# Batch norm in inference form: load and store phases of three tiles in place of two

## The chip, the cores and the metric

The kernel runs on one core of a Trainium2 chip. The metric is the device time of one execution in microseconds (us). The profile's span is about 2 us shorter than the device time of the same execution. The differences that matter are a few tenths of a per cent, so every kernel was run five times or more, beside runs of the kernel before on the same chip. The batches ran on different chips, so kernels of different batches are compared by their ratios to before, or by their traces, and not by their medians.

## The reference

```python
# x: (32, 256, 128, 128) float32; the rest: 256 float32 each
out = gamma * (x - running_mean) / np.sqrt(running_var + 1e-5) + beta
```

The input and the output are 537 MB each. There is one multiply and one add per element, with one scale and one shift per channel.

## The kernel before

The data is cut into 64 tiles of 128 partitions by 16,384 float32 (8.39 MB, 64 KiB in each partition). There are three such buffers. VectorE works on a tile in place.

```python
NBUF = 3
...
    data = ctx.enter_context(tc.tile_pool(name="data", bufs=NBUF))
...
    for i in range(NBUF):
        issue_load(i)                 # nc.sync.dma_start(out=t, in_=xr[i])
    ...                               # scale and shift from the four small inputs
    def compute(i):
        nc.vector.tensor_scalar(out=t[:], in0=t[:], scalar1=scale_t[:, cb:cb+1],
            scalar2=shift_t[:, cb:cb+1], op0=mult, op1=add)      # cut
    def store(i):
        (nc.sync if SINGLE_QUEUE else nc.scalar).dma_start(out=outr[i], in_=t[:])

    K = NBUF - 1
    for b in range((NT + K - 1) // K):
        idxs = [i for i in range(K * b, K * b + K) if i < NT]
        for i in idxs:
            compute(i)
        for i in idxs:
            store(i)
        for i in idxs:
            issue_load(i + NBUF)
```

Loads and stores share one queue, issued by SyncE (`SINGLE_QUEUE` is true). So the DMA engines see three loads, then two stores, two loads, two stores and so on. Each place where a store follows a load in the queue is called a load-to-store switch here; the kernel before has 32.

## Time and profile before

| | before |
|---|---|
| device time, median of the first 3 runs (5 in the end) | 2487.14 us (2487.04) |
| range of the 5 runs | 2486.45 to 2490.18 us |
| the run that was profiled | 2490.18 us, the slowest of them |
| HBM traffic, mean rate | 1073.8 MB, 432 GB/s |

From the page of the profile (kernel before): busy time of the compute engines, then the span in 40 slices with the busy share in tenths and the rate, then the DMA queue.

```profile
DVE 564.7 (23%) x69; ACT 1.6 (0%) x2; POOL 3.2 (0%) x8
...
DMA  9999999999999999999999999999999999999998
GB/s 414 429 438 433 433 429 437 436 430 431 435 436 433 428 437 436 434 428 436 433 437 428 435 435 435 426 437 436 435 427 435 436 438 426 434 437 436 432 431 378
...
q1 hardware_dynamic: 18432, 1073.75, 99.8%
```

VectorE is busy 23% of the time. The DMA engines are busy all the time, but for a little in the last slice. This is a copy with a little arithmetic in its shadow, and its time is that of its 128 tile transfers.

From the timeline of the kernel before (SyncE's queue; start, length, line, what was issued; a load is issued when the store of that buffer has landed):

```profile
82.93 19.66 SPq L48 DMA_DIRECT2D t<-in_x_dram  x2
102.63 28.19 SPq L97 DMA_DIRECT2D out_dram<-t  x2
160.34 19.61 SPq L48 DMA_DIRECT2D t<-in_x_dram  x2
180.00 28.16 SPq L97 DMA_DIRECT2D out_dram<-t  x2
238.40 19.62 SPq L48 DMA_DIRECT2D t<-in_x_dram  x2
...
2409.84 0.34 SPq L48 DMA_DIRECT2D t<-in_x_dram  x1
```

Between 82.93 and 2409.84 lie 30 rounds of two stores and two loads: 77.56 us each.

From its waits (waiter, released by: us in total, times, longest):

```profile
DVE t L86 <- DMA t<-in_x_dram: 1867.9, 63, 49.6
...
SPq L48 <- DMA out_dram<-t: 1484.0, 61, 30.2
SPq L97 <- DVE t L86: 919.2, 33, 46.4
```

VectorE waits three quarters of the time and SyncE nearly all of it. That costs nothing as long as another transfer is queued behind the one that is running.

The trace also records every DMA packet (start and length). Each tile transfer is 8 packets of 64 KiB on each of the 16 DMA engines, and one 4-byte semaphore packet per engine at its end. The records do not name the engine, but on an engine the next packet starts when the last ends, so they can be chained into 16 series (some of the 18,432 links are ambiguous). An undisturbed packet takes 2.418 us for loads and stores alike, and an undisturbed transfer starts 19.319 us after the one before it. That is 8.389 MB / 19.319 us = 434.2 GB/s, next to the 435.2 GB/s that the Trainium skill gives as the ceiling of the SBUF ports, by which these engines reach the on-chip memory ("DMA: Bandwidth & Descriptors", section "Where 436 GB/s comes from").

### The profile page before, as it was taken

Reading aid. Unit: us, or ns where it says so; the run is one execution under the profiler, and the core shown is the slowest. Engines: PE = TensorE matmul, PEld = TensorE weight load, DVE = VectorE, ACT = ScalarE, POOL = GpSimd, SP = SyncE. Lnnn points to the kernel's source line nnn. Section 1 sums busy time; section 2 is a strip of 40 time slices with the busy share of each in tenths; the row PEclk is TensorE's granted clock in tenths of the full one; section 3 lists DMA queues with packets and bytes.
Section 4 is the critical chain, followed back from the end, with each engine's and each line's share of the span. In section 5 each row is a group of like instructions: output and inputs, shape, how many; then the busy total and the mean of one; then the engine's idle time right before and its main releaser. Section 6 shows DMA issues by size and latency. Waiting matters only on the chain.

```text
span 2488.1 us, 378 instructions
## 1 busy us (share of the span) xinstructions
DVE 564.7 (23%) x69; ACT 1.6 (0%) x2; POOL 3.2 (0%) x8
## 2 busy tenths in 40 slices
DVE  2122211222112221122212222121221212212121
ACT  0000000000000000000000000000000000000000
POOL 0000000000000000000000000000000000000000
DMA  9999999999999999999999999999999999999998
GB/s 414 429 438 433 433 429 437 436 430 431 435 436 433 428 437 436 434 428 436 433 437 428 435 435 435 426 437 436 435 427 435 436 438 426 434 437 436 432 431 378
DMA packets 18562, 1073.77 MB, mean 432 GB/s; under 512 B 2176, under 2 KB 2176, under 8 KB 2176
## 3 DMA queue, kind: packets, MB, share of 16 engines
q1 hardware_dynamic: 18432, 1073.75, 99.8%
q0 software_dynamic: 128, 0.00, 0.0%
q14 instruction: 2, 0.02, 0.0%
HBM read 536.88 MB, written 536.87 MB: 432 GB/s over the span
## 4 chain that ended last, share of the span: by engine, by line
DMA 51%; another core or an unknown queue 36%; DVE 11%; SPq 0%; issue 0%; POOL 0%; DVEq 0%; POOLq 0%; PEldq 0%
DMA t<-in_x_dram 48%; DVE t L86 11%; DMA out_dram<-t 2%; DMA t<-in_running_mean_dram 1%; SPq L97 0%; POOL t L56 0%; DVEq L86 0%; POOLq L133 0%; SPq L48 0%; DVE shift_t L81 0%; DVE tmp_t L80 0%; DVEq L80 0%; PEldq L133 0%
## 5 line engine op out<-in xcount | busy, mean ns | idle before, releaser
L86 DVE TENSOR_SCALAR t<-t,scale_t,shift_t 128x16384 f32<-128x16384 f32 x64 | 564.0, 8812 | 1868.0 <-DMA t<-in_x_dram 1867.9
L78 DVE RECIPROCAL tmp_t<-tmp_t 128x2 f32<-128x2 f32 x1 | 0.2, 166 | 13.2 <-ACT tmp_t L71 13.2
L80 DVE TENSOR_TENSOR tmp_t<-t,scale_t 128x2 f32<-128x2 f32 x1 | 0.2, 160 | 7.6 <-DMA t<-in_running_mean_dram 7.6
L71 ACT ACT_TABLE_LOAD x1 | 1.3, 1283 | 12.4 <-DMA t<-in_running_var_dram 12.4
L79 DVE TENSOR_TENSOR scale_t<-t,tmp_t 128x2 f32<-128x2 f32 x1 | 0.2, 160 | 3.2 <-DMA t<-in_gamma_dram 3.2
L56 POOL DMA_DIRECT2D t<-in_running_var_dram x1 | 0.8, 839 | 0.8 <-PEq L133 0.8
L56 POOL DMA_DIRECT2D t<-in_gamma_dram x1 | 0.7, 722 | 0.0
L56 POOL DMA_DIRECT2D t<-in_beta_dram x1 | 0.7, 722 | 0.0
L56 POOL DMA_DIRECT2D t<-in_running_mean_dram x1 | 0.7, 722 | 0.0
L71 ACT ACTIVATE tmp_t<-t,eps_t 128x2 f32<-128x2 f32 x1 | 0.3, 295 | 0.0
L65 DVE MEMSET eps_t<- 128x1 f32 x1 | 0.1, 59 | 0.8 <-PEq L122 0.8
L81 DVE TENSOR_TENSOR shift_t<-t,tmp_t 128x2 f32<-128x2 f32 x1 | 0.2, 160 | 0.0
L122 POOL MEMSET const-bfloat16-1.0<- 128x1 bf16 x1 | 0.1, 96 | 0.0
L122 POOL MEMSET const-uint8-127<- 128x1 uint8 x1 | 0.1, 94 | 0.0
L122 POOL MEMSET const-float32-0.0<- 128x1 f32 x1 | 0.1, 93 | 0.2 <-issue 0.2
L122 POOL MEMSET const-float32-1.0<- 128x1 f32 x1 | 0.1, 93 | 0.0
## 6 DMA issues: line engine op xcount, KB each, us to landing
t<-in_x_dram SPq DMA_DIRECT2D x64, 38.6
out_dram<-t SPq DMA_DIRECT2D x64, 49.9
t<-in_running_var_dram POOLq DMA_DIRECT2D x1, 1.0 KB, 11.1
t<-in_gamma_dram POOLq DMA_DIRECT2D x1, 1.0 KB, 15.2
t<-in_beta_dram POOLq DMA_DIRECT2D x1, 1.0 KB, 19.5
t<-in_running_mean_dram POOLq DMA_DIRECT2D x1, 1.0 KB, 21.6
```

Source lines behind the costliest of these rows:

```text
L56: nc.gpsimd.dma_start(out=t, in_=ap_1d.rearrange("(j p) -> p j", p=P))
L65: nc.vector.memset(eps_t, eps)
L71: nc.scalar.activation(out=tmp_t[:], in_=var_t[:], func=mybir.ActivationFunctionType.Sqrt, bias=eps_t[:], scale=1.0,)
L78: nc.vector.reciprocal(out=tmp_t[:], in_=tmp_t[:])
L79: nc.vector.tensor_mul(out=scale_t[:], in0=gamma_t[:], in1=tmp_t[:])
L80: nc.vector.tensor_mul(out=tmp_t[:], in0=mean_t[:], in1=scale_t[:])
L81: nc.vector.tensor_sub(out=shift_t[:], in0=beta_t[:], in1=tmp_t[:])
L86: nc.vector.tensor_scalar(out=t[:], in0=t[:], scalar1=scale_t[:, cb : cb + 1], scalar2=shift_t[:, cb : cb + 1], op0=mybir.AluOpType.mult, ...
L122: nc = _bacc.Bacc("TRN2", target_bir_lowering=False, num_devices=1)
```

## The change

The intent: fewer changes of direction. All three buffers are loaded, then all three are stored; 22 load-to-store switches in place of 32. Loads, computes, stores, buffers and the queue stay, and `manual_schedule` keeps the instructions in the order written.

```diff
-SINGLE_QUEUE = True
 NBUF = 3
+GROUPS = [3] * 20 + [2, 2]
...
+    ctx.enter_context(tc.manual_schedule())
...
-    K = NBUF - 1
-    for b in range((NT + K - 1) // K):
-        idxs = [i for i in range(K * b, K * b + K) if i < NT]
+    first = 0
+    for g, size in enumerate(GROUPS):
+        idxs = range(first, first + size)
         for i in idxs:
             compute(i)
         for i in idxs:
             store(i)
-        for i in idxs:
-            issue_load(i + NBUF)
+        first += size
+        if g + 1 < len(GROUPS):
+            for i in range(first, first + GROUPS[g + 1]):
+                load(i)
```

More of the change, by code (lines that the diff above doesn't have):

```diff
@@ L33 @@
     NT = N * NCB
+    assert sum(GROUPS) == NT and max(GROUPS) <= NBUF
     params = ctx.enter_context(tc.tile_pool(name="params", bufs=1))
@@ L39, with load @@
     outr = out.rearrange("n (cb p) h w -> (n cb) p (h w)", p=P)
+    ctx.enter_context(tc.manual_schedule())
     tiles = {}
-    loads = {}
-    def issue_load(i):
-        if i >= NT:
-            return
+    def load(i):
         t = data.tile([P, HW], mybir.dt.float32, tag="t")
-        loads[i] = nc.sync.dma_start(out=t[:], in_=xr[i])
+        nc.sync.dma_start(out=t[:], in_=xr[i])
         tiles[i] = t
-    for i in range(NBUF):
-        issue_load(i)
+    for i in range(GROUPS[0]):
+        load(i)
     def load_param(ap_1d):
@@ L96, in store @@
         t = tiles.pop(i)
-        (nc.sync if SINGLE_QUEUE else nc.scalar).dma_start(out=outr[i], in_=t[:])
-    K = NBUF - 1
-    for b in range((NT + K - 1) // K):
-        idxs = [i for i in range(K * b, K * b + K) if i < NT]
+        nc.sync.dma_start(out=outr[i], in_=t[:])
+    first = 0
+    for g, size in enumerate(GROUPS):
+        idxs = range(first, first + size)
         for i in idxs:
@@ L105 @@
             store(i)
-        for i in idxs:
-            issue_load(i + NBUF)
+        first += size
+        if g + 1 < len(GROUPS):
+            for i in range(first, first + GROUPS[g + 1]):
+                load(i)
 _INS = ['x', 'gamma', 'beta', 'running_mean', 'running_var']
```

## The prediction

> **What bounds the kernel now.** The DMA engines. The page gives DMA 9 tenths in 39 of 40 slices, queue q1 99.8% of the 16 engines' span, 432 GB/s mean; VectorE is 23% busy. The Trainium skill, "DMA: Bandwidth & Descriptors", section "Where 436 GB/s comes from", puts the ceiling at 435.2 GB/s; the trace agrees to 1% (inner slices of 426 to 438).
>
> From the trace's DMA packet records: 16,384 packets of 64 KiB, median 2.418 us each, the same for loads and stores; one 8.39 MB tile takes 19.32 us from start to start. 128 transfers x 19.32 = 2473 us. The span is 2488.1, so only about 15 us (0.6%) is anything else: about 2 us before the first packet, about 1 us of slow first packets, small delays, the last completion.
>
> **The avoidable part.** Times over 2.418 us sit almost all at one place: the end of the last load of a phase and the start of the store behind it (summed per engine, 1.6 us over 31 last loads, 2.3 us over 32 first stores). Store-to-load switches show 0.1 us. In wall time (timeline): the first load of a phase is issued at 82.93 and, 30 rounds of two stores and two loads later, at 2409.84: 77.56 us a round, against 4 x 19.32 = 77.28. So about 0.29 us is lost per load-to-store switch.
>
> **What the change does.** The work stays: 64 loads, 64 computes (8.81 us each), 64 stores, same buffers, same queue. By the instruction order, load-to-store switches fall from 32 to 22. Ten x 0.29 = about 2.9 us (estimate), all on the critical path since the DMA engines are.
>
> The fear is a drain, because all three buffers are now loaded before any is stored. I expect none. When the third load lands, two stores are already queued behind it: their computes ended while loads of 19.3 us still ran. The third compute (8.81 us) hides under those stores (38.6 us). When the first store lands, two more are queued while its load is issued; before, one was. The skill, same page, section "Queues, rings and completion order", says each engine consumes descriptors in ring order; the trace agrees (landings 19.3 us apart). The deeper queue also tolerates drift between engines (their last packets end about 9 us apart), worth a microsecond or two at most. VectorE's longest waits grow from 49 to about 68 us and cost nothing. Start and tail stay.
>
> **Prediction.** 2487.1 - 2.9 = 2484.2 us; 8 in 10 between 2481.0 and 2487.2. Faster by over 2%: 0.005 (the floor of 2473 us is only 0.6% away); same: 0.985; slower by over 2%: 0.01.
>
> **What would show it.** Right: DMA still 9 in every slice but the last, mean GB/s up by 0 to 1; VectorE still 564 us; a period of 6 transfers of 115.9 plus about 0.3 us between the first loads of phases; packet excess still only at load-to-store switches, a third fewer. Wrong: a period of 116.5 us or more says the cost goes with the length of a phase, not the number of switches; a slice with DMA well under 9 would be a bubble.
>
> **What would make it wrong.** A cost per switch that grows with the phase's length; the fixed program order adding a wait on SyncE; long phases letting the engines drift further apart, so that the slowest engine's tail eats the gain; run-to-run spread (2486.6 to 2490.2 before) as large as the effect.

## The result, and the profile after

| | before | after |
|---|---|---|
| median of 5 runs | 2487.04 us | 2488.37 us |
| range | 2486.45 to 2490.18 | 2486.35 to 2490.49 |
| the run that was profiled | 2490.18 (span 2488.1) | 2487.72 (span 2485.7) |

The ratio is 1.0003, with a 95% interval of 0.9991 to 1.0016. A ratio is the mean time of one kernel's runs over that of the other's of the same rounds, so it is not quite the ratio of the medians. The gain of 0.12% that was predicted is not there, and the median lies 1.2 us above the predicted range.

From the page of the kernel after:

```profile
DVE 564.7 (23%) x69; ACT 1.6 (0%) x2; POOL 3.2 (0%) x8
...
DMA  9999999999999999999999999999999999999999
GB/s 408 436 439 429 431 438 430 435 435 432 429 438 436 432 431 436 436 427 436 436 432 432 436 437 428 433 438 431 430 439 436 427 437 438 430 431 438 436 432 390
...
q1 hardware_dynamic: 18432, 1073.75, 99.8%
```

No slice ran dry: the feared drain is not there. VectorE's work is the same.

From the timeline of the kernel after (SyncE's queue):

```profile
82.67 39.17 SPq L46 DMA_DIRECT2D t<-in_x_dram  x3
149.65 38.99 SPq L95 DMA_DIRECT2D out_dram<-t  x3
198.75 39.07 SPq L46 DMA_DIRECT2D t<-in_x_dram  x3
...
2291.51 19.66 SPq L46 DMA_DIRECT2D t<-in_x_dram  x2
```

From 82.67 to 2291.51 there are 19 rounds of three stores and three loads, 116.25 us each.

From its waits:

```profile
DVE t L84 <- DMA t<-in_x_dram: 1865.8, 63, 69.0
...
SPq L95 <- DVE t L84: 1455.0, 64, 47.2
SPq L46 <- DMA out_dram<-t: 949.7, 60, 19.1
```

VectorE's longest wait grew from 49.6 to 69.0 us, as foreseen, at no cost.

Now a trap. Taken alone, the two profiles seem to confirm the prediction: 2488.1 us fell to 2485.7, which is 2.4 of the 2.9 us. But the profile of before is that of its slowest run, and that of after is of one of its faster ones. The other runs show no gain.

### The profile page after: what moved, and what is told of

It reads as the page before. It is cut to its first block, busy times and chain, and to the rows that moved or that the text cites. A ratio compares the mean times of both kernels' runs of the same rounds, so it can differ in the third digit from the quotient of the medians.

```text
span 2485.7 us, 377 instructions
## 1 busy us (share of the span) xinstructions
DVE 564.7 (23%) x69; ACT 1.6 (0%) x2; POOL 3.2 (0%) x8
## 4 chain that ended last, share of the span: by engine, by line
another core or an unknown queue 72%; DVE 22%; DMA 4%; issue 0%; DVEq 0%; SPq 0%
DVE t L84 22%; DMA t<-in_x_dram 4%; DVEq L84 0%; SPq L46 0%; SPq L95 0%
```

## The experiments

Fifteen runs of five or six executions each were made, two of them repeats. The theories:

- **A**: every load-to-store switch costs a fixed 0.2 to 0.3 us (the prediction's view), and the first runs were unlucky.
- **B**: the loss goes with bytes or time, not with switches.
- **C**: the fixed program order costs what the switches gain.
- **D**: a switch costs more after a longer phase.
- **E** (formed after the first four runs): the 16 engines start in step; at switches some of them fall behind; once they have drifted apart, further switches cost little. The time is that of the engine furthest behind.
- **F**: the delays fade with time or addresses, not with drift.

### How many switches: 1, 8, 32 and 62

Run `alternate`: one load, one store, in turn.

```diff
-    first = 0
-    for g, size in enumerate(GROUPS): ...
+    compute(0); compute(1); store(0); store(1)
+    for i in range(2, NT):
+        if i + 1 < NT:
+            load(i + 1)
+        compute(i)
+        store(i)
```

> One load, one store, in turn after the first three loads: 62 load-to-store switches in place of 32, same work. Theory A (each switch costs a fixed 0.2 to 0.3 us): +6 to +9 us over before. Theory B (the loss is there per byte or per microsecond of the run, whatever the number of switches): within 1.5 us of before. Theory C (the fixed program order costs the 3 us that the change failed to gain): this kernel has it too, so +3 to +4 us, plus A or B.

Measured: median 2486.71 us (2485.27 to 2488.95), ratio to before 0.9999 (0.9986 to 1.0013). The interval allows at most 3.2 us for thirty more switches, where A asked for 6 to 9: A is wrong as it stands, and the +3 us of C is not seen.

Runs `phase8` and `phase64`: within a phase each buffer is loaded and computed several times, and only its last contents are stored, into every output. Their outputs are wrong, which doesn't matter for the times. The transfers and the VectorE work are the same in number and size.

```diff
-    first = 0 ...
+    first = 0
+    for size in GROUPS:                  # [8] * 8, or [64]
+        idxs = range(first, first + size)
+        for k, i in enumerate(idxs):
+            load(i)                      # into bufs[i % NBUF]
+            if k >= NBUF - 1:
+                compute(i - NBUF + 1)
+        for i in list(idxs)[-(NBUF - 1):]:
+            compute(i)
+        for i in idxs:
+            store(i)                     # from bufs[i % NBUF], in phase64 (i + 1) % NBUF
+        first += size
```

> Phases of eight loads and eight stores through the three buffers (wrong result on purpose), 8 load-to-store switches in place of 32. Theory A: 24 fewer switches, -5 to -7 us against before. Theory B: within 1.5 us of before. A third theory, D (a switch costs more the longer the phase before it): also about 0, and the excess over the bare 2.418 us packet time per switch is several times that of before.

> All 64 loads (each computed), then 64 stores: one load-to-store switch (wrong result on purpose). Theories A and D: -6 to -9 us, near 2479 to 2481 us, and the run-to-run spread shrinks from 4 us to about 1. Theory B: within 1.5 us of before with the same spread, and slow packets everywhere in the trace.

Measured: `phase8` 2484.26 us (2483.90 to 2485.42), ratio 0.9989 (0.9976 to 1.0001); `phase64` 2484.44 us (2484.14 to 2484.64), ratio 0.9988 (0.9976 to 1.0001). The intervals just reach 1, but all ten runs lie below the fastest of the nine runs of before beside them (2486.46). Even with one switch only about 3 us go (0.12% of 2487), and 6 us at most, not the 6 to 9 of A; B, which expected a change of at most 1.5 us, misses too. D expected no gain from `phase8`, and its delay at the last loads was 0.07 us per switch, less than in the kernel before: D falls. The spread of `phase64` shrank to 0.5 us, so with one switch the scatter is nearly gone.

Run `two_fixed`: the kernel before with `manual_schedule` added, nothing else.

```diff
+    ctx.enter_context(tc.manual_schedule())
     tiles = {}
```

> The kernel before with the fixed program order alone, phases of two as they were. Theories A, B and D: the same as before within 1.5 us. Theory C: +3 us or more.

Measured: 2487.21 us (2485.58 to 2488.74), ratio 1.0000 (0.9987 to 1.0012). The +3 us or more of C is not there (the interval ends at +3.0 us).

### Repeats of both kernels

> The changed kernel once more, for its spread and a second trace. Theory A (a fixed 0.2 to 0.3 us per load-to-store switch, first five runs unlucky): median near 2484.5. Theory E (the loss comes while the 16 engines drift apart from their common start, mostly in the first ten or so switches, and is not per switch): 2486 to 2489, as before; in the trace the last load packet before a store is late by about 0.15 to 0.2 us per engine in each of the first ten switches and less than that in the last ten.

Measured: 2487.91 us (2487.12 to 2488.54), ratio to before 0.9992 (0.9978 to 1.0005). Over both batches the changed kernel's ten runs have a mean of 2488.25 us. But the chip of this batch was slower (before had a median of 2488.92 us there), and the interval holds the predicted 0.9988: this batch alone does not separate A from E. Against before on the same chip the means of the changed kernel differ by +1.2 us in the first batch and by -1.8 us here. So a gain of about a microsecond is not excluded. The part of the expectation on fading fails within this kernel: the delays of the last loads sum to 1.43 us per engine over the first ten switches and to 1.40 over the last ten.

Run `three_sched` is the changed kernel with the `manual_schedule` line taken out.

```diff
-    ctx.enter_context(tc.manual_schedule())
     tiles = {}
```

> The changed kernel without the fixed program order. All theories that leave the order aside (A, E): the same as the changed kernel within 1.5 us. Theory C (the fixed order costs): 3 us less.

Measured: 2488.04 us (2486.51 to 2490.61), ratio to before 0.9995 (0.9982 to 1.0007), as with it (its mean is 1.1 us under that of before on this chip). No effect of the order shows.

> The kernel before once more, for a second trace. If the 0.29 us per round of the first profile is typical: (period of two stores and two loads) again 77.55 to 77.60 us. If it was the mark of a slow run: 77.40 to 77.50 us, that is 0.1 to 0.2 us per switch, and lag of the slowest engine at the end 4 to 7 us in place of 9.2. In both cases the delays of the first ten switches are larger than those of the last ten.

Measured: 2487.12 us (2486.58 to 2491.17), ratio 1.0001 (0.9989 to 1.0013). This time the profiled run was a short one, 2486.58 us. From its timeline (SyncE's queue):

```profile
82.71 19.75 SPq L48 DMA_DIRECT2D t<-in_x_dram  x2
...
2406.74 0.34 SPq L48 DMA_DIRECT2D t<-in_x_dram  x1
```

Thirty rounds in 2324.03 us are 77.47 us each, against 77.56 in the first profile. So a switch cost 0.19 us here, not 0.29. The timeline gives for all six profiles of the two orders (loss is the period less 4 or 6 times 19.319 us):

| run | period, us | lost per switch | times its switches |
|---|---|---|---|
| before (profiled run 2490.18) | 77.564 | 0.29 | 32: 9.2 |
| before_again (2486.58) | 77.468 | 0.19 | 32: 6.1 |
| two_fixed (2487.21) | 77.486 | 0.21 | 32: 6.7 |
| after (2487.72) | 116.255 | 0.34 | 22: 7.5 |
| after_again (2487.91) | 116.257 | 0.34 | 22: 7.5 |
| three_sched (2487.99) | 116.278 | 0.36 | 22: 8.0 |

This is the answer to the main question. Fewer switches cost more each, and the product stays at 6 to 8 us, apart from the one profile of the 2490.18 us run.

### Who loses the time: the engines that are already behind

From the packet records, for each kernel: the loss between the end of the 4th transfer and that of the 128th, beyond 124 x 19.319 us, for the mean of the 16 engines and for the slowest; and the lag of the slowest engine behind the first at the end.

| run | switches | loss, mean engine | loss, slowest engine | lag at the end |
|---|---|---|---|---|
| phase64 | 1 | 3.1 us | 3.6 us | 1.6 us |
| phase8 | 8 | 2.0 | 3.1 | 4.0 |
| after, after_again, three_sched | 22 | 3.5, 3.3, 3.1 | 6.7, 6.9, 7.0 | 5.6, 6.5, 7.0 |
| before, before_again, two_fixed | 32 | 4.1, 3.1, 3.8 | 8.9, 5.8, 6.4 | 9.2, 5.6, 5.0 |
| alternate | 62 | 4.4 | 6.1 | 3.6 |

The mean engine's loss hardly moves. From 32 to 22 switches it falls by about 0.4 us (means of three), not by 2.9. The time of the kernel is the slowest engine's, and that one does not follow the number of switches at all from 22 upward. In `phase64` the 3.1 us is another loss: nothing in the last load packet, but 2.9 us in packets all over the run, nearly all of them less than 50 ns late.

The loss sits in a single packet: the last of the eight of the last load before a store. In the profile of before these 512 packets are 3.6 us late per engine in sum, out of 4.0 us for all packets after the first transfer. And it falls on some engines only. Eight engines in the lead were late by 12 ns per switch on average, the eight behind them by 213 ns. (The split is weaker elsewhere: 43 and 132 ns in before_again, 64 and 140 in two_fixed, 85 and 193 in the kernel after.) Two switches of that run (lag behind the first engine, and how late the last load packet was):

```
16th switch: eight engines within 0.3 us: 0 to 2 ns late
             lags 1.2 1.7 3.7 4.4 4.8 5.3 5.4 6.2 us: 267 730 684 727 803 761 720 726 ns late
29th switch: eight engines within 0.4 us: 0 to 3 ns late
             lags 4.7 5.3 7.1 7.9 8.4 8.5 8.8 9.6 us: all 0 ns late
```

In this run the same engines are hit switch after switch, their lag adds up, and late in the run it mostly stops. Sums of these delays per engine in the first ten switches and in the last ten: before_again 1.67 and 0.04 us; two_fixed 1.68 and 0.74; before 1.28 and 0.78; alternate 2.17 and 0.25. The ten switches that the change takes away are thus in effect ten of the cheap ones: with 22 switches the run ends while the engines are still drifting (1.08 to 1.76 us in the first ten, 1.08 to 1.40 in the last ten, over the three runs).

The slowest engine shows it directly. With 32 switches its loss was 7.2, 5.8 and 5.7 us (before, before_again, two_fixed) once the 22nd switch was passed, and 8.9, 5.8 and 6.4 us at the end: the last ten switches cost 1.7, 0.0 and 0.7 us, not 2.9. The changed kernel, which has 22 switches in all, lost 6.7 to 7.0 us, as much as the others had lost by their 22nd or more.

### Put the engines back in step

Run `resync_alt`: the alternating kernel, but after tile 31 no load is issued until the last store has landed (tile 32 takes the buffer of tile 31), so the queue drains once and all engines start together again. The result is right.

```diff
+R = 32
+    def buf(i):  # from tile R on the buffers are shifted: R takes that of R - 1
+        return bufs[(i if i < R else i - 1) % NBUF]
...
+    for lo, hi in ((0, R), (R, NT)):
+        if lo:
+            for i in range(lo, lo + NBUF):
+                load(i)
+        compute(lo); compute(lo + 1); store(lo); store(lo + 1)
+        for i in range(lo + 2, hi): ...     # as in alternate, up to hi
```

> One load and one store in turn, with the DMA queue drained once, after tile 31, so that the engines start in step again. In the trace of the kernel without the drain the delays of the last load packets sum to 2.2 us per engine over the first ten switches and to 0.25 us over the last ten. Theory E: after the drain the delays come back (over 1 us in the ten switches that follow it, under 0.6 in the ten before it), engine lag falls to under 0.5 us and grows again to 3 us; time +4 to +6 us over the kernel without the drain (2 to 2.5 us of drain, the rest a second lag paid for). Rival F (the delays fade for a reason that goes with time or addresses): no delays after the drain, time +2 to +2.5 us.

Measured: 2498.77 us (2496.29 to 2500.62), ratio to before 1.0035 (1.0023 to 1.0048); `alternate` had 0.9999, so the drain costs about 0.36%, or 9 us, more than was expected. From stretches of `resync_alt` (stretch, length, busy us of VectorE, ScalarE and GpSimd, granted clock, DMA share, GB/s), the drain in the middle one:

```profile
1150.00:1200.00 50.00, 8.81 (x1) 0.00 (x0) 0.00 (x0) 1.00 1.00 435
1200.00:1250.00 50.00, 8.81 (x1) 0.00 (x0) 0.00 (x0) 1.00 0.89 380
1250.00:1300.00 50.00, 17.62 (x2) 0.00 (x0) 0.00 (x0) 1.00 1.02 440
```

The DMA share of 0.89 over 50 us is 5.5 us lost, in part because the engines in front had to wait for the last. By the packet records the lag was 5.7 us before the drain, 0.5 right after it, and 8.1 at the end. The delays of the last load packets sum to 0.18 us per engine over the ten switches before the drain and to 2.04 us over the ten after it (under 0.6 and over 1 were expected). That bears out E against F: the delays come back after the drain. But 1.2 us of the 2.04 fall at the first switch after it, where all 16 engines were 1.1 to 1.4 us late and not only those behind; nothing like it stands at the first switch of the run, and E does not explain it. Without that switch the mean engine lost 0.18 us in the 20 transfers up to the 64th and 0.94 us in the 20 transfers from the 67th. The time was under-estimated in part for this, in part because both lags turned out larger than in the run without the drain (3.6 us at its end).

### Put them out of step from the start

Run `stagger_alt`: the alternating kernel, with a few rows of tile 2 loaded first, to give some engines extra packets. The Trainium skill, "DMA: Bandwidth & Descriptors", section "Why a DMA increments its semaphore by 16 and not by 1", says that a DMA runs on the largest number of engines up to 16 that divides the slowest dimension. The trace agrees: 10 and 5 rows add 15 packets of 64 KiB (16,399 in place of 16,384) and 15 semaphore packets (2,063 in place of 2,048).

```diff
+    t = data.tile([P, HW], mybir.dt.float32, tag="t")
+    nc.sync.dma_start(out=t[0:10], in_=xr[2][0:10])
+    nc.sync.dma_start(out=t[16:21], in_=xr[2][16:21])
-    for i in range(NBUF):
+    for i in range(NBUF - 1):
         load(i)
+    nc.sync.dma_start(out=t[:], in_=xr[2])
```

> One load and one store in turn, with two extra small transfers first (10 and 5 rows of 64 KiB) that put 10 engines one packet and 5 of them two packets behind the others: the lag of 2.4 and 4.8 us is there from the start. Theory E: few delays at the first ten switches (under 1 us summed per engine in place of 2.2), lag stays near 5 us, time within 2 us of the kernel without them although up to 4.8 us of transfer was added. Rival (the delays have nothing to do with the engines being in step): 2.2 us of delays as without, and time +3 to +5 us.

Measured: 2499.86 us (2499.76 to 2499.90), ratio to before 1.0040 (1.0028 to 1.0053). By the ratios that is 10 us over `alternate`, where at most 2 were expected, and it is lost at the start (the 4th transfer ended at 98.5 us, in `alternate` at 81.6): from stretches of the run,

```profile
0.00:50.00 50.00, 9.52 (x6) 1.58 (x2) 3.18 (x8) 1.00 0.97 300
50.00:100.00 50.00, 17.62 (x2) 0.00 (x0) 0.00 (x0) 1.00 1.00 434
```

the first 50 us moved 300 GB/s, with packets of 8 to 9 us in place of 2.4. After that the run is the smoothest of all. Lags of 0, 1.6 and 4.1 us (6, 5 and 5 engines) stood from the 4th transfer on and hardly changed but for one engine, and the mean engine lost 0.20 us over 124 transfers and 62 switches, where `alternate` lost 4.4 (the slowest engine lost 2.2 and 6.1). The five times lie within 0.14 us of each other. Switches between engines that are out of step in this way were free (the delays of the last load packets sum to less than 0.1 us over all 62), and the scatter is gone with the delays. `alternate` came by itself to nearly the same groups at its end: 0, 1.5 to 2.1 and 3.4 to 3.6 us.

Four more runs spread the extra rows over the partitions (`t2[0:120:12]`, 10 rows, and `t2[1:121:24]`, 5 rows; in `stag2_after` `t2[0:128:16]` alone, 8 rows), to make the start cheaper. The edit is otherwise that of `stagger_alt`, made in the changed kernel, the kernel before and the alternating one.

> The changed kernel with 15 extra rows of 64 KiB first, spread over the partitions: ten DMA engines one packet behind, five of them two (lags near 0, 2.4 and 4.8 us). Theory E (a load-to-store switch costs only while the engines are in step): the mean engine's excess over 19.319 us per transfer, from the fourth transfer to the last, falls from 3.1 to 3.5 us to under 1; spread between runs falls under 0.5 us (it was 0.05 us in the run with such a lag and one load, one store in turn). Time: if the extra rows cost 3 to 5 us, and not 15 as when they all lay on neighbouring partitions, 2482 to 2486 us. Rival A (fixed cost per switch): excess stays 3 us or more, time +4 us.

> The changed kernel with 8 extra rows: eight engines one packet (2.4 us) behind, two groups of eight. Theory E says less delay than without; whether two groups are enough to end it is open: excess between 0.5 and 2.5 us, time 2482 to 2487 us. Rival A: excess 3 us or more, time +2.4 us.

> The kernel before with the same 15 extra rows. Theory E: excess under 1 us in place of 4, and the same time as the changed kernel with them within 1 us, since its ten more switches cost nothing once the engines are out of step. Rival A: 3 us slower than the changed kernel with the extra rows.

> One load and one store in turn with the same 15 extra rows, spread over the partitions. Theory E: excess near 0.3 us as in the run with neighbouring rows, and the same time as the other two with 15 rows within 1 us, though it has 62 switches. Rival A: 9 us and 12 us slower than those.

| run | median us | ratio to before | lag, 4th transfer | loss, mean engine | loss, slowest |
|---|---|---|---|---|---|
| stag3_after | 2491.22 | 1.0022 (1.0009 to 1.0035) | 3.1 us | 1.7 us | 2.9 us |
| stag2_after | 2494.04 | 1.0024 (1.0010 to 1.0037) | 2.2 | 5.3 | 7.7 |
| stag3_before | 2492.52 | 1.0020 (1.0007 to 1.0032) | 2.8 | 2.4 | 5.7 |
| stag3_alt | 2490.76 | 1.0014 (1.0001 to 1.0026) | 3.0 | 0.9 | 3.1 |

The start was cheaper than with neighbouring rows (the 4th transfer of `stag3_alt` ended at 88.9 us, that of `stagger_alt` at 98.5), but not cheap enough: none beats either kernel. With 15 rows the mean engine's loss fell in all three orders (from 3.3 to 1.7, from 3.7 to 2.4, from 4.4 to 0.9 us), and against A the three kernels with 22, 32 and 62 switches lie within 2 us, the one with most switches in front. Yet the loss stayed above the 1 us expected in two of them, and the five times of `stag3_after` spread over 4.9 us, where under 0.5 was expected; the lags that arose were two blurred groups (10 or 11 engines in front, 5 behind), not the three meant. Two clean groups of eight, 2 us apart, made it worse: 5.3 us. So "out of step" alone is not enough; which pattern of lags is free is not settled.

### Two queues

```diff
-SINGLE_QUEUE = True
+SINGLE_QUEUE = False
```

`three_two_queues` does the same in the changed kernel (`nc.scalar.dma_start` in `store`).

> The kernel before with its own switch SINGLE_QUEUE = False: stores on the scalar queue, loads on the sync queue. No store waits behind a load, so packets of the two directions alternate on each engine all the time. If the loss is per change of direction (theory A at packet scale): slower, by tens of us or more. Theory E: engines are out of step soon, so within 3 us of before, unless the queue runs dry, since a load must wait for a store that now takes twice as long: then slices with DMA below 9.

> The changed kernel with its stores on the scalar queue. As for two_queues; with phases of three the two queues overlap more, so no slice should run dry: within 3 us of the changed kernel by theory E, tens of us slower by theory A at packet scale.

Measured, six runs each: `two_queues` 2490.38 us (2483.32 to 2502.25), ratio 1.0012 (0.9993 to 1.0031); `three_two_queues` 2485.53 us (2482.49 to 2510.35), ratio 1.0007 (0.9975 to 1.0039). The Trainium skill, "DMA: Bandwidth & Descriptors", section "Issuing engines are not separate DMA queues", says that DMAs of several issuers run on the same 16 engines and interleave. The trace agrees (each queue holds 50% of the engines' time), and the median packet still takes 2.418 us. In the profiled run of `two_queues` (2483.32 us) about 85% of an engine's packets follow one of the other direction, and all time over 2.418 us, that of the slow first packets included, sums to 2.5 us per engine. So a change of direction between packets of two queues costs next to nothing by itself: A falls at the scale of packets too. The best runs beat every right kernel with one queue by 2 to 3 us (the best of those took 2485.27), the worst lose 15 to 22. From stretches of the profiled run of `three_two_queues`, one of its two long ones (2506.01 us):

```profile
2440.00:2460.00 20.00, 2.27 (x1) 0.00 (x0) 0.00 (x0) 1.00 1.04 449
2460.00:2480.00 20.00, 7.90 (x1) 0.00 (x0) 0.00 (x0) 1.00 0.26 111
2480.00:2504.00 24.00, 0.92 (x1) 0.00 (x0) 0.00 (x0) 1.00 0.82 352
```

Between 2460 and 2480 us three quarters of the engines' time is idle: 15 engines had brought the last tile by 2454 us, one only at 2471.6, 26 us after the first, and the last compute could not start before. In this run one engine came some 20 us after the others by half of the run. It is a lag as above, but larger; that it has the same cause is not shown. This is no version to choose, as its mean is not better.

## Why the prediction was wrong

- **The DMA engines bound the kernel, and nothing runs dry.** Right: DMA is at 9 in every slice after the change, VectorE still takes 564 us, and its longest wait is 69.0 us (68 was said).
- **The place of the loss.** Right: the last load packet before a store, and nothing at store-to-load switches. The part put on the store's first packets was a mistake of counting by start time; chained by engine, those too are last load packets, of engines that are behind.
- **A period of 115.9 plus about 0.3 us.** It came out (116.25), but it proved nothing, since the other side of the comparison was not 0.29. That it came out was luck.
- **"Ten x 0.29 = about 2.9 us (estimate), all on the critical path".** This is the step that failed. First, the size: 0.29 us came from the profile of a run of 2490.18 us, and the sum started from the median, 2487.1. In two other profiles of the same order it is 0.19 and 0.21. Second, the form: the loss is not so much per switch. With 22 switches it is 0.34 to 0.36 each, with 32 0.19 to 0.29, and the total is 7.5 to 8.0 against 6.1 to 9.2 us. The last ten of 32 switches cost the slowest engine 1.7, 0.0 and 0.7 us in three profiles, not 2.9. It is the lag that the slowest of 16 engines gathers while the engines drift apart. This lag grows over the first ten to twenty-odd switches and then little more, so the switches taken away were cheap ones. In the mean engine's packets the change saved about 0.4 us, lost in the spread of the runs.
- **Drift.** The prediction named "long phases letting the engines drift further apart, so that the slowest engine's tail eats the gain" among what could make it wrong, and gave it a microsecond or two in the right direction. The drift was the main term: 5.6 to 9.2 us of lag at the end in the first two profiles. That longer phases cause more of it is not shown (5.6 to 7.0 us after, 5.0 to 9.2 before).
- **"The floor of 2473 us".** With a single switch the time is 2484.44 us. Small delays in long runs of one direction (about 3 us for the mean engine), start and end remain. At most 3 us were to be had from switches at all.

That the loss is not so much per switch is shown (`alternate`, `phase64`, and the last ten switches above). The account by drift is shown in part: the drain brought the delays back and `stagger_alt` had none, but `stag2_after`, out of step from the start, had more. Two things stay open: why an engine that is behind loses up to 0.8 us in its last load packet at one switch and nothing at another, and which pattern of lags stops it. None of the variants computes the right result and beats both kernels beyond the spread of the runs.

## What to carry to other kernels

When a term of the sum is taken from one profile, check which of the runs that profile was, and take the starting time from that same run; a comparison of two single profiles can show a gain of 2 us that does not exist. A loss found at some kind of event is not yet a price per event: change the number of events both ways, and far, before multiplying. A transfer over 16 engines ends with the slowest of them, so ask for the lag between engines as well as for the busy share, which read 9 in nearly every slice throughout.

## What the Trainium skill lacked or had wrong

- "DMA: Bandwidth & Descriptors" says that the engines of one DMA finish independently, but not by how much they drift. Here the slowest was 1.6 us behind at the end with one load-to-store switch, 3.6 to 9.2 us with 22 to 62 on one queue, and about 26 us in a run with two queues. The run-to-run spread of five runs was 0.5 us with one switch and 1.4 to 4.6 us with 22 or 32.
- No page has the late last load packet before a store: 65 to 140 ns on average over all engines and switches in runs of 22 to 62 switches without extra rows, up to 0.8 us and more on engines that are behind.
- No page gives the price of changing direction on a DMA engine. At packet scale next to none shows: the median packet took 2.418 us on one queue and on two, where about 85% of the packets follow one of the other direction.
- "HBM Reference", section "Specifications (TRN2)", gives about 425 GB/s for a core that streams alone. Here the kernels before and after, loads and stores together, ran at 432 GB/s; the measurement decides.
